# Layer 0 opens by pairs of channel tiles, and its modulation products run in four column groups of the array

## The chip, the cores and the metric

The kernel runs on one core of a Trainium2 chip. The metric is the device time of one execution in microseconds (us). Engines are named as in the profile: PE (matrix products), PEld (weight loads of PE), DVE and ACT (vector and scalar work), POOL, and SP, which issues most DMAs.

## The reference, cut to what matters

Two layers run over 1024 latent and 256 context tokens, 1024 channels wide. Each layer first derives a shift, a scale and a gate per channel from a conditioning vector, once for the latents (c) and once for the context (c_ctx), and modulates the normalised tokens with them. The result h feeds all the layer's projections: attention, a convolution branch, a recurrent branch (RG-LRU), and merge gates.

```python
shift, scale, gate = jnp.split(jax.nn.silu(c) @ w_ada[l] + b_ada[l], 3, axis=-1)
shift_c, scale_c, gate_c = jnp.split(jax.nn.silu(c_ctx) @ w_ada[l] + b_ada[l], 3, axis=-1)
h = layer_norm(x) * (1.0 + scale[:, None]) + shift[:, None]
hc = layer_norm(ctx) * (1.0 + scale_c) + shift_c
q, k, v, g_att, u_conv, g_conv, x_lru, g_lru = split_in_proj(h @ w_in[l])
...
g = jax.nn.sigmoid(h @ w_gate + b_gate).reshape(h.shape[:-1] + (N_BRANCH, D_MODEL))
```

`w_ada[l]` is 1024 x 3072, so silu(c) and silu(c_ctx) are two rows against 24 column tiles of 128: tiles 0 to 7 are the shift, 8 to 15 the scale, 16 to 23 the gate. These are the modulation products.

## The kernel before, in words

**Splitting.** The layer's large products keep float32 accuracy by splitting both operands into a high part in a reduced float format (hi) and the rest (lo), and running three products: hi by hi, hi by lo, lo by hi. A weight tile (`Wt`, lines 321 to 344) is 512 KB: SP loads it into one of two slots named `raw` (`NWL` is 2), ACT copies it to `whi`, DVE subtracts to get `wlo`. The slot is free once DVE has read it. The modulated tokens are held transposed, channels on partitions, as `hchi`/`hclo` (context, 256 columns) and `hlhi`/`hllo` (two latent tiles of 512 columns): eight channel tiles of 128 each. In the code these three token tiles are NT_C, NT_0 and NT_1.

**The opening** (`emit_h0`, lines 429 to 504). An explicit list `order` sets the recorded order. For the modulation of layer 0, 16 tiles `raw0` of w_ada (shift and scale, 2 KB runs) are loaded, and `ada_rows` multiplies them unsplit in float32: 2 stationary columns (`cs`: c and c_ctx), 512 moving columns, eight channel tiles accumulated into one PSUM tile `pa`, four groups in all. `ada_fin` copies the 2 x 512 result to `arow` on ACT and turns it into columns with four small products against `sel`. Ten tiles of x (two of context, eight of latents, 128 tokens each) are loaded and normalised (`norm_x`: two statistics, an aggregate and small operations on DVE, a power on POOL, one pass on ACT). `modulate` transposes one channel tile of one token tile on PE, applies scale and shift on ACT (`hf`), and splits it on ACT and DVE.

**The order of the work.** The recorded program is put in order per engine by the framework's scheduler; every engine then runs its own list strictly in order, and so does the DMA issue of SP. In `phase1` a driver with a cost table (`Driver`, `Meter`) decides in which order the streams of the layer are recorded; nine streams run side by side, among them `lru_in` (products of the recurrent branch), `gates` (24 merge-gate tiles) and `att_values`.

**Later modulation products** (`ada_pair`, lines 391 to 403). The stream `gates` of layer 0 calls it 16 times, once after each of the first 16 gate tiles, for two column tiles each: the four gate pairs of layer 0 and the twelve pairs of layer 1. It takes two `Wt` units (so two loads, two ACT splits, two DVE splits) and runs 16 products with 4 stationary columns (`csr`, the hi and lo of `cs`) and 256 moving columns.

Of the kernel before, what the change touches and what calls it, by code (L numbers as in the profile page):

```python
# [8 lines left out]
F32 = mybir.dt.float32  # L9
# [3 lines left out]
ALU = mybir.AluOpType  # L13
# [176 lines left out]
def kernel(  # L190
# [25 lines left out]
    PR = ctx.enter_context(tc.tile_pool(name="padr", bufs=1, side="right"))  # L216
    pad(PR, 320, "padr")
# [39 lines left out]
    def load_rows(l, get):  # L257
# [3 lines left out]
        for off, n, src in (  # L261
# [11 lines left out]
            sp.dma_start(out=ra[off:off + n], in_=src)  # L273
        sp.dma_start(out=rb[0:CK * 4], in_=conv_dw_w[l].rearrange("k (r p) -> (k r) p", p=128))
# [81 lines left out]
    cs = K.tile([128, KD, 2], F32, tag="cs", name="cs")  # L356
    csr = K.tile([128, KD, 4], F32R, tag="csr", name="csr")
    sel = K.tile([4, 2], F32, tag="sel", name="sel")
    dve.tensor_tensor(out=sel, in0=ident[0:4, 0:2], in1=ident[0:4, 2:4], op=ALU.add)

    def load_c():
        rows = SM.tile([128, 128], F32, tag="crow", name="crow")
        sp.dma_start(out=rows[0:8], in_=c[0].rearrange("(r p) -> r p", p=128))
        sp.dma_start(out=rows[8:16], in_=c_ctx.rearrange("(r p) -> r p", p=128))
        t = SM.tile([128, 128], F32, tag="crow2", name="crow2")
# [6 lines left out]
        split(cs, csr[:, :, 0:2], csr[:, :, 2:4])  # L372
# [18 lines left out]
    def ada_pair(l, jj, row):  # L391
# [9 lines left out]
        for w in ws:  # L401
            w.free()
# [20 lines left out]
    hT, hr = {}, {}  # L423

# [3 lines left out]

    def emit_h0(R, P):
        tiles = [(ctxt, 0), (ctxt, 128)] + [(x, 128 * i) for i in range(8)]  # L430
        raws, xt = {}, {}
        nts = (NT_C, NT_0, NT_1)

        def load_x(i):
            t = R.tile([128, 2, 512], F32, tag="raw0", name="x0", bufs=17).rearrange("p a b -> p (a b)")
            sp.dma_start(out=t, in_=tiles[i][0][0, tiles[i][1]:tiles[i][1] + 128, :])
            xt[i] = t

        def load_ada(g, q):
            raws[g, q] = R.tile([128, 2, 512], F32, tag="raw0", name="raw0", bufs=17)  # L440
            sp.dma_start(out=raws[g, q], in_=w_ada[0][q * 256:q * 256 + 256, g * 512:g * 512 + 512].rearrange(
                "(k p) n -> p k n", p=128))

        rows_ = {}

        def ada_rows(g, q):
            if q == 0:
                rows_[g] = P.tile([128, 512], F32, tag="p0", name="pa", bufs=4)
            for k in range(2):
                pe.matmul(out=rows_[g][0:2], lhsT=cs[:, q * 2 + k, :], rhs=raws[g, q][:, k, :],  # L450
                          start=(q == 0 and k == 0), stop=(q == 3 and k == 1))
            if q == 3:
                ada_fin(0, [g * 4 + i for i in range(4)], rows_[g], 2,
                        R.tile([128, 512], F32, tag="hf0", name="arow", bufs=5))
# [8 lines left out]
        def modulate(j, nt):  # L463
# [5 lines left out]
            hf = R.tile([128, 512], F32, tag="hf0", name="hf0", bufs=5)  # L469
# [3 lines left out]
            if j < (4, 4, 6)[ti]:  # L473
                act.activation(out=hi, in_=hf[:, 0:n], func=AF.Copy)
            else:
                dve.tensor_copy(hi, hf[:, 0:n])
            dve.tensor_tensor(out=lo, in0=hf[:, 0:n], in1=f32(hi), op=ALU.subtract)

        load_c()
# [4 lines left out]

        def rows_tile():
            return R.tile([128, 128], F32, tag="rows", name="rows", bufs=2)

        order = [("a", 0, 0), ("a", 0, 1), ("a", 0, 2), ("r",), ("a", 2, 0), ("a", 0, 3), ("a", 2, 1), ("a", 2, 2),
                 ("a", 2, 3), ("x", 0), ("x", 1), ("a", 1, 0), ("a", 1, 1), ("a", 1, 2), ("a", 1, 3), ("a", 3, 0),
                 ("a", 3, 1), ("a", 3, 2), ("a", 3, 3), ("m", NT_C, 0), ("m", NT_C, 4), ("x", 2), ("x", 3),  # L490
                 ("x", 4), ("x", 5), ("x", 8), ("m", NT_0, 0), ("m", NT_0, 4), ("x", 6), ("x", 9), ("x", 7),
                 ("m", NT_1, 0), ("m", NT_1, 4)]
        for what, *v in order:
            if what == "m":
                for j in range(v[1], v[1] + 4):
                    modulate(j, v[0])
            elif what == "r":
                load_params(0, *load_rows(0, rows_tile))
            elif what == "a":
                load_ada(*v)  # L500
                ada_rows(*v)
            else:
                load_x(*v)
                norm_x(*v)
# [20 lines left out]
    def phase1(l, R, RH):  # L525
        last = l == DEPTH - 1
        full = [NT_0, NT_1] if last else [NT_C, NT_0, NT_1]
        allt = [NT_C, NT_0, NT_1]
        lo_t = C if last else 0
        p, d = prm[l], drv[l]  # L530
        sl, hl_, pl_ = Pool_(NS), Pool_(NHF), Pool_(4)
        state = dict(lru=False, late=False)

        def slot(name, dt=F32):
# [950 lines left out]
```

## Time and profile before

| | |
|---|---|
| median of 3 runs | 2303.75 us (2302.42 to 2304.94) |
| profiled execution, its own time | 2301.99 us |
| its span, first to last instruction | 2300.2 us |
| mean granted clock of PE | 0.991 of full speed |
| PE busy | 2248.0 us (98%) |
| DVE busy | 1681.1 us (73%) |
| ACT busy | 1005.0 us (44%) |

The time is read against PE: it is busy nearly throughout, so a change counts by the PE time that it adds or removes, and by the stretches in which PE waits or runs at a lower granted clock. A float32 product shows as two MATMUL rows in the profile, each with a weight load of its own.

### The profile page before, as it was taken

To read this page: it belongs to the slowest core of one execution; us is meant where nothing else is said; L and a number is where in the kernel's file an instruction comes from. 1 tells how busy PE (TensorE), PEld (TensorE's weight loads), DVE (VectorE), ACT (ScalarE), POOL (GpSimd) and SP (SyncE) were. 2 spreads that over 40 slices of the span, in tenths; PEclk is the share of its full clock that TensorE was granted. 3 is DMA by queue.
4 is the path that set the end of the run, shared out by engine and by line. 5 is a ranking of instruction groups with operands and counts; after the bars stand their busy time and mean duration, and the time that the engine had idled before them with its cause. 6 is when DMAs were issued, how large, how long until landed. Compare 5 with 4: busy or idle time off the path is not lost.

```text
span 2300.2 us, 29966 instructions
## 1 busy us (share of the span) xinstructions
PE 2248.0 (98%) x11344; PEld 1870.5 (81%) x11344; DVE 1681.1 (73%) x2453; ACT 1005.0 (44%) x1642; POOL 86.0 (4%) x140
## 2 busy tenths in 40 slices
PE   7999999999999999999999999999999999999998
PEld 2888888888888787888888788888888878878886
DVE  5579967868959875544678749879778797765667
ACT  3555563245444475421132544665243446642110
POOL 1000000000000111000001100000000011000002
PEclk8999999999999999999999999999999999999999
DMA  7223323433334232555461312224433334347532
GB/s 276 77 74 101 115 70 125 147 108 113 100 108 140 81 117 88 187 166 178 144 222 65 103 53 79 77 78 144 130 102 100 88 110 133 124 141 223 162 127 92
DMA packets 270945, 279.90 MB, mean 122 GB/s; under 512 B 19768, under 2 KB 199888, under 8 KB 270800
## 3 DMA queue, kind: packets, MB, share of 16 engines
q1 hardware_dynamic: 242288, 226.06, 31.6%
q10 hardware_dynamic: 28512, 51.92, 6.4%
q8 instruction: 89, 1.46, 0.3%
q14 instruction: 56, 0.46, 0.1%
HBM read 203.04 MB, written 74.88 MB: 121 GB/s over the span
## 4 chain that ended last, share of the span: by engine, by line
PE 90%; DVE 4%; ACT 2%; DMA 2%; issue 1%; SPq 0%; POOLq 0%; POOL 0%; ACTq 0%; DVEq 0%
PE ps L73 83%; PE yp L73 3%; PE pt L73 2%; PE pa L73 2%; DVE acc L73 1%; DVE P L73 1%; DMA qd<-qd 1%; DVE wlo L73 0%; DVE pl L73 0%; ACT whi L73 0%; PE p L73 0%; DVE xp L73 0%; DMA raw<-in_w_in_dram 0%; ACT hf L73 0%; DMA yst<-yd 0%
## 5 line engine op out<-in xcount | busy, mean ns | idle before, releaser
L73 PE MATMUL ps<-hlhi,whi 128*128 128x512 f32 x1728 | 681.5, 395 | 2.5 <-DVE pl L73 1.5
L73 PE MATMUL ps<-hllo,whi 128*128 128x512 f32 x1728 | 677.8, 392 | 0.0
L73 PE MATMUL ps<-hlhi,wlo 128*128 128x512 f32 x1728 | 677.1, 393 | 0.0
L73 PEld LDWEIGHTS ps<-hlhi,wlo 128*128 128x128 f32 x1728 | 325.8, 189 | 67.9 <-issue 0.4
L73 PEld LDWEIGHTS ps<-hlhi,whi 128*128 128x128 f32 x1728 | 326.3, 189 | 66.8 <-DVE pl L73 2.9
L73 PEld LDWEIGHTS ps<-hllo,whi 128*128 128x128 f32 x1728 | 326.2, 189 | 62.0 <-issue 0.2
L73 DVE SCALAR_TENSOR_TENSOR acc<-u,cwt,acc 128x1296 f32<-128x1296 f32 (+1 forms) x240 | 342.1, 1425 | 2.2
L73 ACT ACTIVATE whi<-raw 128x1024 fp32r<-128x1024 f32 x180 | 190.0, 1058 | 339.8 <-PE ps L73 307.2
L73 DVE TENSOR_TENSOR wlo<-raw,whi 128x1024 fp32r<-128x1024 f32 x180 | 220.6, 1226 | 96.5 <-ACT whi L73 93.5
L73 PE MATMUL ps<-yy,whi 128*128 128x512 f32 (+1 forms) x960 | 271.4, 368 | 2.5 <-DVE m L73 2.5
L73 PEld LDWEIGHTS ps<-yy,whi 128*128 128x128 f32 x960 | 173.7, 188 | 33.3 <-DVE m L73 3.1
L73 PE MATMUL ps<-yy,wlo 128*128 128x512 f32 (+1 forms) x480 | 176.5, 368 | 0.0
L73 ACT ACTIVATE ph<-pt 128x512 fp32r<-128x512 f32 x160 | 94.2, 593 | 144.2 <-PE pt L73 142.7
L73 DVE TENSOR_TENSOR pl<-pt,ph 128x512 fp32r<-128x512 f32 x160 | 109.3, 686 | 59.2 <-ACT ph L73 57.7
L73 PE MATMUL ps<-hchi,whi 128*128 128x256 f32 x480 | 135.9, 283 | 1.3 <-ACT whi L73 0.6
L73 PE MATMUL ps<-hchi,wlo 128*128 128x256 f32 x480 | 135.5, 282 | 1.0 <-DVE wlo L73 1.0
L73 PE MATMUL ps<-hclo,whi 128*128 128x256 f32 x480 | 134.8, 281 | 0.0
L73 ACT ACTIVATE P<-P,nm 128x640 f32<-128x640 f32 (+1 forms) x128 | 101.9, 798 | 73.1 <-DVE nm L73 72.5
L73 DVE CUSTOM_DVE_ANT_0 P<-ps,m_mid,nsink 128x640 f32<-128x640 f32 (+1 forms) x112 | 93.6, 860 | 43.6 <-PE ps L73 42.0
L73 ACT ACTIVATE tg<-ps,drv 128x512 f32<-128x512 f32 (+1 forms) x120 | 76.5, 638 | 69.0 <-PE ps L73 68.5
L73 PEld LDWEIGHTS ps<-yy,wlo 128*128 128x128 f32 x480 | 90.5, 188 | 15.2
L73 PE MATMUL pt<-ident,P 128*128 128x128 f32 x640 | 98.0, 273 | 3.3 <-DVE pl L73 1.4
(205 smaller groups left out, 3397.6 us busy)
## 6 DMA issues: line engine op xcount, KB each, us to landing
raw<-in_w_in_dram SPq DMA_DIRECT2D x60, 512.0 KB
raw<-in_w_ada_dram SPq DMA_DIRECT2D x48, 512.0 KB
raw<-in_w_gate_dram SPq DMA_DIRECT2D x48, 512.0 KB
th<-tg ACTq DMA_DIRECT2D x96, 256.0 KB
thl<-th SPq DMA_DIRECT2D x96, 256.0 KB
yd<-gs ACTq DMA_DIRECT2D x48, 256.0 KB
yst<-yd SPq DMA_DIRECT2D x48, 256.0 KB
raw<-in_w_branch_dram SPq DMA_DIRECT2D x24, 512.0 KB
```

Source lines behind the costliest of these rows:

```text
L73: return f(*a, **k)
```

## The change

It has three parts.

1. **The opening is reordered.** Loads of x come first, the parameter rows are loaded from ACT's DMA queue (`load_rows(..., act)`), and w_ada is read in four groups of two channel tiles (shift and scale together, 256 columns each, so 1 KB runs, eight loads of 256 KB per group). The list `order` is gone: group after group, `modulate` runs for two channel tiles of all three token tiles.
2. **Four accumulations of the layer begin in the opening** (`share`): the first `lru_in` weight tile against all three token tiles, and the first gate tile against NT_0, each three products per channel tile, as soon as that channel tile is there. `phase1` then finds these four PSUM tiles finished and only evacuates them. All of the high parts in `modulate` are now made on ACT.
3. **All modulation products are unsplit float32 in four column groups.** `csz` holds `cs` padded with zeros to 32 columns; channel tile k goes to columns 32(k mod 4) of the array, so four partial sums stand on four groups of 32 partitions, and `sel` (now 128 x 2) adds them. In `ada_pair` this removes the two `Wt` units: the pair loads its two tiles (`araw`) straight into the two slots `raw` and reads them there, so a slot is free only when PE has run the pair's products.

```diff
@@ emit_h0, lines 440 to 543 of the changed kernel
+        def load_ada(g):
+            for q in range(4):
+                raws[g, q] = R.tile([128, 2, 2, 256], F32, tag="raw0", name="raw0", bufs=18)
+                src = w_ada[0][q * 256:q * 256 + 256, 0:2 * D].rearrange("(k p) (t n) -> p k t n", p=128, t=2)
+                for k in range(2):
+                    sp.dma_start(out=raws[g, q][:, k], in_=src[:, k, :, g * 256:g * 256 + 256])
+        def ada_cols(g):
+            pa = P.tile([128, 512], F32, tag="p0", name="pa", bufs=4)
+            for k in range(KD):
+                c_ = k % 4
+                pe.matmul(out=pa[32 * c_:32 * c_ + 32], lhsT=csz[:, k, :],
+                          rhs=raws[g, k // 2][:, k % 2].rearrange("p t n -> p (t n)"), start=(k < 4), stop=(k >= 4),
+                          tile_position=(0, 32 * c_))
+            row = R.tile([128, 512], F32, tag="arow", name="arow", bufs=1)
+            act.activation(out=row, in_=pa, func=AF.Copy)
+            for i in range(4):
+                pe.matmul(out=pa[:, 2 * i:2 * i + 2], lhsT=row[:, i * 128:i * 128 + 128], rhs=sel4, start=True, stop=True)
...
+        def share(j, nt):
+            for kind in ("lru", "gate"):
+                if (kind, nt[0]) in first:
+                    w, ps = first[kind], first[kind, nt[0]]
+                    for i, (a, b) in enumerate(((0, 0), (0, 1), (1, 0))):
+                        pe.matmul(out=ps[:, 0:nt[2]], lhsT=w[a][:, j, :], rhs=hT[0, nt[0]][b][:, j, :],
+                                  start=(j == 0 and i == 0), stop=(j == KD - 1 and i == 2))
...
+        for g in range(4):
+            if 0 < g < 3:
+                load_ada(g + 1)
+            if g:
+                ada_cols(g)
+            for nt in nts:
+                if g == 0 and nt is NT_1:
+                    for i in range(6, 10):
+                        norm_x(i)
+                for j in (2 * g, 2 * g + 1):
+                    modulate(j, nt)
+                    share(j, nt)
@@ ada_pair
-        ws = [Wt(w_ada[l][i * 512:i * 512 + 512, jj * 128:jj * 128 + 256].rearrange("(k p) n -> p k n", p=128), 4, 256)
-              for i in range(2)]
         ps = psum()
-        for k in range(KD):
-            for v in range(2):
-                pe.matmul(out=ps[0:4, 0:256], lhsT=csr[:, k, :], rhs=ws[k // 4][v][:, k % 4, :],
-                          start=(k == 0 and v == 0), stop=(k == KD - 1 and v == 1))
-        ada_fin(l, [jj, jj + 1], ps, 4, row)
+        for i in range(2):
+            for g in range(4):
+                pe.matmul(out=ps[32 * g:32 * g + 32, 0:256], lhsT=csz[:, 4 * i + g, :], rhs=raws[i][:, g, :],
+                          start=(i == 0), stop=(i == 1), tile_position=(0, 32 * g))
+        ada_fin(l, [jj, jj + 1], ps, 128, row)
```

Two places show how the order moves. The first is PE in the opening of the changed kernel, at the second group of modulation products: `p` are transposes of x tiles (x_202 is the first context tile, x_334 to x_340 the last four of the latents), `pa` the modulation products, `ps` products of the layer.

```order
L73 MATMUL p_446<-ident,x_334 128x128
L73 MATMUL p_458<-ident,x_334 128x128
L73 MATMUL pa<-raw_261,cs 32x512 x2
L73 MATMUL pa<-raw_264,cs 32x512 x2
L73 MATMUL pa<-raw_267,cs 32x512 x2
L73 MATMUL pa<-raw_270,cs 32x512 x2
L73 MATMUL p_499<-ident,x_202 128x128
L73 MATMUL p_499<-ident,x_204 128x128
L73 MATMUL ps<-hlhi,whi 128x512
```

In the kernel before, the modulation products stand ahead of nearly all transposes; now the second group of four stands behind the transposes of the first of the last four latent tiles. On DVE of the changed kernel the factor `nb_410` that this x tile's normalisation needs (x_334) stands behind the statistics of x_338, two tiles later:

```order
L73 TENSOR_SCALAR rs_407<-mv_405 128x1
L73 BN_STATS st_424<-x0_338 128x6 x2
L73 BN_AGGR mv_416<-st_413 128x2
L73 SCALAR_TENSOR_TENSOR nb_410<-mv_405,rs_407 128x1
L73 BN_AGGR mv_427<-st_424 128x2
```

So the list of PE waits at this place for the load of x_338. The second place is the seventh modulation pair of layer 0, first on SP of the changed kernel (`araw` are the pair's two tiles, `raw` the layer's weight tiles; all share two slots), then on PE:

```order
L397 DMA araw_3150<-in_w_ada_dram 128x4x256
L397 DMA araw_3152<-in_w_ada_dram 128x4x256
L965 DMA vd0_142<-vh_2934 128x512
L965 DMA vd1_143<-vh_2938 128x512
L330 DMA raw_3188<-in_w_in_dram 128x8x128
L330 DMA raw_3194<-in_w_gate_dram 128x8x128
```

```order
L73 MATMUL ps_3032<-hlhi_185,wlo_2616 128x512
L73 MATMUL ps_3155<-araw_3150,cs_155 32x256 x4
L73 MATMUL ps_3155<-araw_3152,cs_155 32x256 x4
L73 MATMUL ps_3168<-ident_76,pj_3007 128x128 x4
L73 MATMUL ps_3155<-sel_157,arow_3154 128x2 x2
L73 MATMUL ps_3214<-hchi_179,whi_3190 128x256
L73 MATMUL ps_3214<-hclo_180,whi_3190 128x256
L73 MATMUL ps_3214<-hchi_179,wlo_3191 128x256
```

The load of `raw_3188` takes the slot of `araw_3150`, which PE's four products of that tile set free; `whi_3190` and `wlo_3191` are its split, and PE reads them nine small instructions later.

## Rows read from the trace of the kernel before

**Rows 1.** The page, part 1: busy time, share of the span and instructions.
```profile
PE 2248.0 (98%) x11344; PEld 1870.5 (81%) x11344; DVE 1681.1 (73%) x2453; ACT 1005.0 (44%) x1642; POOL 86.0 (4%) x140
```

**Rows 2.** Stretches of the opening: length, busy time per engine, PEclk, DMA share, GB/s.
```profile
0.00:10.00 10.00, 3.87 (x6) 0.78 (x7) 1.56 (x11) 1.81 (x3) 2.80 (x15) 1.00 0.49 164
10.00:20.00 10.00, 10.00 (x24) 1.90 (x23) 4.70 (x29) 0.80 (x2) 0.00 (x0) 1.00 0.88 314
20.00:30.00 10.00, 9.98 (x35) 3.16 (x34) 4.02 (x17) 2.96 (x3) 1.07 (x2) 1.00 1.04 393
30.00:40.00 10.00, 10.00 (x33) 2.91 (x32) 3.78 (x10) 0.59 (x1) 0.55 (x1) 1.00 1.05 389
50.00:60.00 10.00, 8.05 (x41) 6.88 (x40) 8.23 (x24) 10.00 (x15) 2.29 (x3) 0.55 0.52 157
```

**Rows 3.** Timeline of PE, opening: start, length, tile, shape, count, idle and releaser.
```profile
6.38 7.70 PE L73 MATMUL pa<-raw,cs 128*2 128x512 f32 x12 [0.27 <-DVE cs L73]
14.38 7.03 PE L73 MATMUL pa<-raw,cs 128*2 128x512 f32 x16
...
36.35 1.05 PE L73 MATMUL pa<-sel,arow 2*128 2x2 f32 x8
...
46.28 1.14 PE L73 MATMUL p<-ident,x 128*128 128x128 f32 x4 [1.76 <-ACT hf L73]
...
73.73 0.60 PE L73 MATMUL p<-ident,x 128*128 128x128 f32 x4
```

**Rows 4.** One stretch, instructions that read hchi, then those that read hlhi.
```profile
55.60:74.40 18.80, 7.38 (x32) 5.88 (x32) 0.42 (x1) 0.00 (x0) 0.91 0.30 92
55.60:74.40 18.80, 6.51 (x19) 3.78 (x20) 10.43 (x19) 5.86 (x10) 0.91 0.30 92
```

**Rows 5.** Groups on PE: tiles, shape, count, busy us, mean ns, idle before.
```profile
L73 PE MATMUL pa<-raw,cs 128*2 128x512 f32 x64 | 31.0, 633 | 0.3 <-DVE cs L73 0.3
L73 PE MATMUL ps<-whi,csr 128*4 128x256 f32 x128 | 31.6, 278 | 0.0
L73 PE MATMUL ps<-sel,arow 4*128 4x2 f32 x64 | 9.6, 251 | 0.2 <-ACT arow L73 0.2
```

**Rows 6.** Timeline of PE: two rows of one modulation pair, then the layer's products.
```profile
97.59 0.28 PE L73 MATMUL ps<-wlo,csr 128*4 128x256 f32 x1
...
98.29 0.28 PE L73 MATMUL ps<-wlo,csr 128*4 128x256 f32 x1
...
75.10 0.39 PE L73 MATMUL ps<-hlhi,wlo 128*128 128x512 f32 x1
...
76.02 0.39 PE L73 MATMUL ps<-hlhi,whi 128*128 128x512 f32 x1
```

**Rows 7.** Timeline of DVE and ACT: statistics and normalisation of one tile of x.
```profile
37.71 1.23 DVE L73 BATCH_NORM_STATS2 st<-x 128x6 f32<-128x512 f32 x2
...
42.36 1.23 ACT L73 ACTIVATE x<-x,nb,rs 128x1024 f32<-128x1024 f32 x1
```

**Rows 8.** Split of a weight tile: instructions, ns min/median/max, first and last start.
```profile
L73 ACT ACTIVATE whi<-raw x180: 1039/1061/1081, 46.6 to 2211.0; 128x1024 fp32r<-128x1024 f32 x180
L73 DVE TENSOR_TENSOR wlo<-raw,whi x180: 1207/1220/1996, 48.4 to 2215.9; 128x1024 fp32r<-128x1024 f32 x180
```

**Rows 9.** Timeline of SP and ACT: one weight load, from issue to its split.
```profile
95.45 0.37 SPq L332 DMA_DIRECT2D raw<-in_w_in_dram  x1
...
100.25 1.06 ACT L73 ACTIVATE whi<-raw 128x1024 fp32r<-128x1024 f32 x1 [0.21 <-DMA raw<-in_w_in_dram]
```

**Rows 10.** PE's longest wait from 75 to 745 us; that stretch by engine.
```profile
PE yp L73 <- ACT ph L73: 3.7, 4, 1.9
...
95.00:745.00 650.00, 642.51 (x3562) 544.97 (x3561) 525.21 (x692) 310.96 (x501) 2.01 (x17) 1.00 0.35 110
```

**Rows 11.** A gap of PE between the layers, and the granted clock around it.
```profile
1313.76 1.97 PE L73 MATMUL ps<-ident,xp 128*128 128x128 f32 x8 [3.87 <-ACT hf L73]
...
1310.00:1320.00 10.00, 6.24 (x22) 5.32 (x23) 6.18 (x11) 9.70 (x23) 1.13 (x5) 0.66 0.19 68
```

More of the change, by code (lines that the diff above doesn't have):

```diff
@@ L423 @@
     hT, hr = {}, {}
+    GATES = list(range(16, 24)) + list(range(8, 16)) + list(range(8))
     def alloc_h(ti, n):
@@ new lines, in ada_cols @@
+        def ada_cols(g):
[9 more added lines that the diff above has]
+                pe.matmul(out=pa[:, 2 * i:2 * i + 2], lhsT=row[:, i * 128:i * 128 + 128], rhs=sel4, start=True, stop=True)
+            for part in range(2):
+                jj = 8 * part + 2 * g
+                bias = prm[0][:, P_ADA + jj:P_ADA + jj + 2].unsqueeze(2).to_broadcast([128, 2, 2])
+                dve.scalar_tensor_tensor(out=ada[0][:, jj:jj + 2, :],
+                                         in0=pa[:, 4 * part:4 * part + 4].rearrange("p (m s) -> p m s", s=2),
+                                         scalar=float(part), in1=bias, op0=ALU.add, op1=ALU.add)
@@ L483, in emit_h0 @@
                 pad(H, 64, "padh2")
[L485 to L504, printed above, removed]
+        ra, rb = load_rows(0, lambda: R.tile([128, 128], F32, tag="rows", name="rows", bufs=2), act)
+        for i in range(2):
+            load_x(i)
+        load_ada(0)
+        load_params(0, ra, rb)
+        for i in range(2, 6):
+            load_x(i)
+        for i in range(2):
+            norm_x(i)
+        first["lru"] = wcols(w_in[0], O_XL)
+        load_ada(1)
+        ada_cols(0)
+        for i in range(2, 6):
+            norm_x(i)
+        for i in range(6, 10):
+            load_x(i)
+        first["gate"] = wcols(w_gate[0], GATES[0] * 128)
+        for nt in nts:
+            first["lru", nt[0]] = psum()
+        first["gate", 1] = psum()
+        for g in range(4):
[3 more added lines that the diff above has]
+                ada_cols(g)
+            for nt in nts:
+                if g == 0 and nt is NT_1:
+                    for i in range(6, 10):
+                        norm_x(i)
+                for j in (2 * g, 2 * g + 1):
+                    modulate(j, nt)
+                    share(j, nt)
     class Pool_:
@@ L531, in phase1 @@
         sl, hl_, pl_ = Pool_(NS), Pool_(NHF), Pool_(4)
+        if first:
+            pl_.take(4)
         state = dict(lru=False, late=False)
@@ L619, in lru_in @@
                 for nt in allt:
-                    yield from gemm_nt(w, nt, evac)
+                    if ("lru", nt[0]) in first:
+                        yield "act"
+                        evac(first.pop(("lru", nt[0]))[:, 0:nt[2]], nt)
+                        pl_.give()
+                    else:
+                        yield from gemm_nt(w, nt, evac)
                 w.free()
@@ L1101, in att_out @@
                 yield from gating(0, j, get, 1.0)
-        gorder = list(range(16, 24)) + list(range(8, 16)) + list(range(8))
+        gorder = GATES
         def gate_nt(w, j, nt):
@@ L1117, in gates @@
         def gates():
-            ws = {}
+            ws = {0: first.pop("gate")} if l == 0 else {}
             def fetch(i):
```

82 lines of the change are left out of this document (39 added, 43 removed).

## The prediction, made before the changed kernel ran

> **What bounds the kernel now.** I read first the page's busy times: PE is busy 98% of the span, DVE 73%, ACT 44% [rows 1]. So the layer's products set the time, and a change pays by PE time saved or by gaps closed. Then the opening in stretches: for 40 us the DMAs are the tight resource, 164 and 314 GB/s in the first two stretches, then 393 and 389 at a busy share over 1 [rows 2]; PE counts as busy there, but with modulation products. Its timeline shows what they cost: 16 rows take 7.03 us, so (7.03 - 0.59) / 15 = 0.43 us a row, and there are 64 rows for 32 products [rows 3, 5]. Each float32 product is thus two passes of 0.43 us. The first twelve rows took 7.70 us, where 12 x 0.43 is 5.2: the clock came up on the way, 2.5 us lost [rows 3].
>
> The last transposes of x end at 74.3 us [rows 3]. By then PE had run products of the layer: 32 readers of hchi, which are two in three, so 48 of 256 columns, and likewise 29 of 512 [rows 4]. A 256-column row starts every (98.29 - 97.59) / 6 = 0.117 us, a 512-column row every 0.92 / 4 = 0.23 [rows 6]; that makes 5.6 + 6.7 = 12.3 us of useful work. The opening therefore costs 74.3 - 12.3 = **62 us** in which no product of the layer ran. After it PE hardly waits: from 95 to 745 us it is idle 7.5 of 650 us [rows 10].
>
> **The change, part by part.**
>
> *The price of the four column groups* is the unknown on which most hangs; no row before uses them. Bounds: all four at once (a group of eight products, 16 passes, takes 4 passes' time), or one after another (16). I take 9: a product is two passes on the same columns, so its second pass waits for its first; rows of PE start in order, so the next product's first pass can only run beside that second one. Sixteen passes then take 9 slots of 0.43 us at 512 columns, of 0.215 at 256 (half the columns).
>
> The Trainium skill (TensorE: Matmul & The Clock Gate, Part 3) says that matmuls start and end in program order, which is the step I lean on; it also measured 2.38 times for three column tiles, which speaks for a gain near the first bound. No run here shows either.
>
> *The opening.* Until the last x tiles are there PE can do little. In the new order PE's second modulation group stands behind transposes of x_334, these behind its normalisation, whose factor stands on DVE behind the statistics of x_338. Up to x_338, 9 tiles of x, one weight tile and two modulation groups are loaded: (9 + 1) x 0.52 + 2 x 2.1 = 9.4 MB. Before, 20 us brought 4.8 MB and the rest would come at 0.39 MB per us [rows 2], so at 32 us; but eleven small loads no longer stand on SP among the large ones, and at the full rate from 2.5 us on it is 27. I take 28. Statistics (1.23), small operations (0.5) and the normalisation (1.23) follow [rows 7]: 31 us. From there PE has, beside products of the layer:
> - three modulation groups of 9 x 0.43: 11.6 us (bounds 5.2 and 20.6);
> - 68 of 80 transposes at (0.60 - 0.27) / 3 = 0.11 [rows 3]: 7.5 us;
> - three sets of `sel` products at 1.05 [rows 3]: 3.2 us;
> - a clock that must rise once more: PE had granted 0.55 where it waited in the opening [rows 2]; 2.5 us as above;
> - two waits for ACT's `hf` of 1.76 us as shown [rows 3], since the third and fourth groups' factors come late in PE's list: 3.5 us.
>
> That is 28.3 us. Of the products begun in the opening, 12 rows on the first two channel tiles (6 of 256, 6 of 512 columns: 2.1 us) lie before 31 us. So the opening now costs 31 - 2.1 + 28.3 = 57.2 us against 62: **-5 us** (ends: -12 and +4). The 19 us of products that `share` brings forward are no gain in themselves; they only fill gaps. ACT's pass for the remaining high parts and the parameter loads lie beside the DMA stretch; ACT, busy all of 50 to 60 us before [rows 2], is the next to be late, which is why I keep the two waits.
>
> *The 16 pairs.* Before, 16 rows of 0.117: 1.87 us. Now 9 x 0.215 = 1.93: **+1 us** in all. The `sel` products stay at four rows a pair [rows 5]. Bounds: 4 slots, -16 us; 16 slots, +25 us.
>
> *ACT and DVE work removed*: 32 splits, 1.06 us on ACT and 1.22 on DVE each [rows 8], 34 and 39 us. PE's idle time in that stretch is 7.5 us in all, the longest group of waits 3.7 us behind ACT [rows 10]; so between 0 and -7.5, and I take **-2 us**, since most waits belong to attention, not to queues.
>
> *The wait that is added.* A pair holds both raw slots until PE has run it, and the next weight load on SP stands behind. A weight load took from its issue at 95.45 to its split at 100.25, 4.8 us [rows 9]; with 1.06 and 1.22 for the split [rows 8] the first product can start 5.9 us after the slot is free, the third 7.1. At the seventh pair PE has only four passes' worth of the pair (1.0), four transposes (0.45) and two `sel` products (0.5) before it reads that weight: 1.9 us. PE stands for 4 us, and 1 more for `wlo`. Following all 16 pairs down PE's list in the same way, one more is short (4.6 us of work, 2 us of wait); the others have 6.6 us or more. **+7 us** (ends: 0 if the scheduler's order hides more than I see; 12, since a PE gap of 3.87 us elsewhere went with a granted clock of 0.66 over 10 us [rows 11]).
>
> *Sum:* -5 + 1 - 2 + 7 = +1 on the profiled execution's 2301.99 (0.1% under the median, inside the spread of the runs): **2303 us**, no change. A measurement of this kernel can tell about 0.2%, 4.6 us, from nothing.
>
> **The rivals.**
>
> 1. *Four groups truly at once.* Three opening groups save 3 x 5 x 0.43 = 6.5 us, 16 pairs 16 x 5 x 0.215 = 17 us: 2303 - 23.5 = **2279**. For it: the four groups touch different columns and different partitions of PSUM. Against it: the two passes of each product on the same columns. The Trainium skill's 2.38 of 3 (the page and part named above) is of this kind.
>
> 2. *No overlap at all* (the side of slower). Then 16 passes stay 16: 3 x 7 x 0.43 = 9 us in the opening and 16 x 7 x 0.215 = 24 us in the pairs: **2336**. It decides from about 11 slots in place of 9 on: two slots more are 2 x (3 x 0.43 + 16 x 0.215) = 9.5 us, which is slower. For it: every row of the trace so far runs one pass after another. Against it: separate columns need nothing from each other.
>
> 3. *Each change between whole array and column groups empties PE.* A 256-column row lasts 0.278 us, one starts every 0.117 [rows 5, 6]; the difference, 0.16 us, is what an emptied pipeline loses. Two changes for each of 16 pairs and 4 groups: 40 x 0.16 = 6.4 us: **2309**. For it: nothing in the trace, where rows of 4 and of 128 stationary columns follow each other at the same pace. The Trainium skill (TensorEngine Tiling (Array Packing), Key Properties) states that changing the tiling mode drains the engine; no run here shows it.
>
> **How the numbers follow.** Chances: the forecast 0.38, rival 1 0.32, rival 2 0.17, rival 3 0.13. The forecast's own range, from its ends, is 2291 to 2316; rival 1 has 2268 to 2290, rival 3 2300 to 2320, rival 2 2322 to 2350. A range from 2270 to 2322 leaves out nearly all of rival 2 and the best edge of rival 1, about 2 in 10. Faster by over 0.2%: nearly all of rival 1 and a quarter of the forecast, 0.42. Within 0.2%: nearly half of the forecast and a quarter of rival 3, 0.21. Slower: the rest, 0.37.
>
> **What would show it.** In the changed profile: eight column-group products of a pair spread over 1.9 us (0.9 for rival 1, 3.4 for rival 2), with the next product of the layer 0.1 us behind (0.25 or more for rival 3); the second opening group starting near 31 us and the last transposes of x near 72; products of the layer done by then worth 14 us or more; a PE wait of 4 us or more on `whi` or `wlo` right behind the seventh pair, where before there was none. A last transpose at 65 us or earlier, or a pair under 1.5 us, breaks my sum downward; a pair over 2.5 us, or waits on weights of over 12 us in all, breaks it upward.

## The result, and the profile after

| | before | after |
|---|---|---|
| median of the runs beside each other | 2303.09 us (2300.58 to 2304.94, 4 runs) | 2333.68 us (2332.05 to 2335.93, 4 runs) |
| span of the profiled execution | 2300.2 us | 2333.4 us |
| mean granted clock of PE | 0.991 | 0.982 |

The change makes the kernel slower: the ratio is 1.0131, with an interval of 1.0117 to 1.0145. The forecast was no change. The busy times of the page, which answer to [rows 1]:

```profile
PE 2243.2 (96%) x11344; PEld 1865.7 (80%) x11344; DVE 1644.5 (70%) x2417; ACT 982.6 (42%) x1619; POOL 82.7 (4%) x139
```

PE is busy 4.8 us less than before, but idle 2333.4 - 2243.2 = 90.2 us where it was idle 52.2. So the time went into waits, not into work. The first place to look is the opening, in the stretches of [rows 2] that differ most:

```profile
20.00:30.00 10.00, 4.24 (x14) 2.62 (x14) 8.94 (x44) 7.61 (x10) 2.16 (x4) 0.50 1.09 361
30.00:40.00 10.00, 6.93 (x24) 2.68 (x24) 8.20 (x23) 6.31 (x8) 2.16 (x4) 0.50 1.09 349
```

PE waits there at half the clock, as foreseen. The timeline of PE shows the second group of modulation products, a later group, and the last transposes of x [rows 3]:

```profile
36.36 0.69 PE L73 MATMUL p<-ident,x 128*128 128x128 f32 x2 [2.02 <-ACT x L73]
36.98 3.53 PE L73 MATMUL pa<-raw,cs 128*32 128x512 f32 x16
...
49.17 1.92 PE L73 MATMUL pa<-raw,cs 128*32 128x512 f32 x16 [0.29 <-ACT hf L73]
...
69.83 1.68 PE L73 MATMUL p<-ident,x 128*128 128x128 f32 x12 [0.48 <-DVE ada L73]
```

The second group starts at 37 us, not 31. DVE shows why: the statistics of the first of the last four tiles (x_334) begin at 29.9 us, when its load lands, and the factor that ACT needs is made 5 us later, behind the statistics of two more tiles and two splits, where 1.7 us was priced.

```profile
29.91 1.29 DVE L73 BATCH_NORM_STATS2 st<-x 128x6 f32<-128x512 f32 x2 [0.23 <-DMA x<-in_x_dram]
...
34.93 0.10 DVE L73 SCALAR_TENSOR_TENSOR nb<-mv,rs 128x1 f32<-128x1 f32 x1
```

At full clock a group of 16 passes takes 1.92 us; the forecast had 3.9. The errors happen to cancel: the last transposes end at 71.5 us. By then 12 of the rows that read `hchi` and 36 that read `hlhi` have started, which in the way of [rows 4] are 18 x 0.117 + 54 x 0.23 = 14.5 us of the layer's products. The opening costs 57.0 us, against 62 before. That is no loss.

A modulation pair, in the timeline of PE [rows 6]:

```profile
100.24 0.28 PE L73 MATMUL ps<-hchi,whi 128*128 128x256 f32 x1
100.45 1.07 PE L73 MATMUL ps<-araw,cs 128*32 128x256 f32 x16
101.45 0.38 PE L73 MATMUL ps<-hclo,whi 128*128 128x256 f32 x1
101.67 0.28 PE L73 MATMUL ps<-hchi,wlo 128*128 128x256 f32 x1
```

Sixteen passes take 1.00 us from the first start to the next product's start; before it was 1.87, and 1.93 was forecast. A row of 256 columns otherwise starts every 0.117 us, so each edge of the pair costs 0.21 - 0.12 = 0.09 and 0.22 - 0.12 = 0.10 us more. Inside the pair the rows start in four waves of four, 0.22 to 0.24 us apart; within a wave each starts 7 ns behind the one before. The first wave (a view of 100.4 to 100.6 us):

```profile
100.45 0.42 PE L73 MATMUL ps<-araw,cs 128*32 128x256 f32 x4
```

The pairs are cheaper than before, so they aren't the loss either.

The loss is in the rest of layer 0's first phase. Here is the stretch from 75 to 1000 us, by engine, of the kernel before and then of the changed one (columns as in rows 2):

```profile
75.00:1000.00 925.00, 909.68 (x4981) 772.29 (x4980) 692.42 (x974) 450.32 (x758) 26.23 (x41) 0.99 0.35 111
```

```profile
75.00:1000.00 925.00, 880.96 (x4830) 741.47 (x4829) 639.82 (x912) 411.56 (x706) 23.70 (x38) 0.98 0.34 103
```

PE is idle 15.3 us before and 44.0 us after. The changed kernel's waits of PE in this stretch (total us, times, longest) answer to [rows 10]:

```profile
PE pt L73 <- ACT P L73: 7.7, 2, 4.7
PE ps L73 <- ACT whi L73: 6.1, 3, 3.7
PE ps L73 <- ACT qh L73: 5.3, 1, 5.3
PE yp L73 <- ACT ph L73: 5.2, 7, 1.6
PE yp L73 <- DVE pl L73: 4.9, 7, 1.6
```

The longest of the kernel before in the same stretch are shorter, and no wait of `pt` on `P` or of `ps` on `qh` is in its list:

```profile
PE yp L73 <- ACT ph L73: 4.8, 6, 1.9
PE yp L73 <- DVE pl L73: 2.8, 3, 2.4
```

One of the changed kernel's waits is the one that was foreseen. The timeline of all engines behind the seventh pair:

```profile
361.50 1.07 PE L73 MATMUL ps<-araw,cs 128*32 128x256 f32 x16
...
362.20 0.38 SPq L330 DMA_DIRECT2D raw<-in_w_in_dram  x1
...
366.27 1.06 ACT L73 ACTIVATE whi<-raw 128x1024 fp32r<-128x1024 f32 x1 [2.69 <-DMA raw<-in_w_in_dram]
...
367.38 0.39 PE L73 MATMUL ps<-hchi,whi 128*128 128x256 f32 x1 [3.69 <-ACT whi L73]
...
368.64 0.58 PE L73 MATMUL ps<-hchi,wlo 128*128 128x256 f32 x1 [0.76 <-DVE wlo L73]
```

Four us for `whi` and one for `wlo` were forecast; 3.69 and 0.76 came. A lower clock follows, as it did behind the gap of [rows 11]; in this view PE's busy time is followed by PEclk, DMA share and GB/s:

```profile
367.00:379.00 12.00, 9.99 (x54) 0.72 0.69 210
```

But the other waits belong to attention (`P`, `qh`, `ph`), whose instructions the change doesn't touch. Why they wait longer is what the runs had to find.

### The profile page after: what moved, and what is told of

It is laid out like the page before. It is cut to its first block, busy times and chain, and to the rows that moved or that the text cites. A ratio compares the mean times of both kernels' runs of the same rounds, so it can differ in the third digit from the quotient of the medians.

```text
span 2333.4 us, 29872 instructions
## 1 busy us (share of the span) xinstructions
PE 2243.2 (96%) x11344; PEld 1865.7 (80%) x11344; DVE 1644.5 (70%) x2417; ACT 982.6 (42%) x1619; POOL 82.7 (4%) x139
## 4 chain that ended last, share of the span: by engine, by line
PE 84%; DVE 6%; DMA 4%; ACT 3%; issue 2%; SPq 0%; POOL 0%; POOLq 0%; ACTq 0%; DVEq 0%
PE ps L73 79%; PE yp L73 3%; PE pt L73 2%; DVE acc L73 1%; DMA yst<-yd 1%; DMA raw<-in_w_gate_dram 1%; DMA raw<-in_w_ada_dram 1%; DVE wlo L73 1%; ACT whi L73 1%; DVE P L73 1%; DMA raw<-in_w_in_dram 0%; ACT P L73 0%; ACT hf L73 0%; DVE pl L73 0%; PE pa L73 0%
## 5 line engine op out<-in xcount | busy, mean ns | idle before, releaser
L73 ACT ACTIVATE whi<-raw 128x1024 fp32r<-128x1024 f32 x148 | 156.4, 1058 | 315.1 <-PE ps L73 240.5
L73 DVE TENSOR_TENSOR wlo<-raw,whi 128x1024 fp32r<-128x1024 f32 x148 | 181.8, 1229 | 90.1 <-ACT whi L73 87.1
L73 DVE TENSOR_TENSOR pl<-pt,ph 128x512 fp32r<-128x512 f32 x160 | 109.0, 685 | 58.8 <-ACT ph L73 57.2
L73 PEld LDWEIGHTS pt<-ident,P 128*128 128x128 f32 x640 | 80.2, 143 | 35.0 <-ACT P L73 8.3
```

Source lines behind the costliest of these rows:

```text
L73: return f(*a, **k)
```

## The experiments

In every group the kernel before ran on the same chip; its median was between 2303.6 and 2304.8 us. "PE idle" is 925 us less PE's busy time from 75 to 1000 us in that kernel's trace.

| run | what it is | median us | ratio to before (interval) | PE idle |
|---|---|---|---|---|
| e1_own | change, pairs in slots of their own | 2314.76 | 1.0048 (1.0033 to 1.0063) | 32.2 |
| e1b_half | change, pairs in quarter tiles of another pool | 2316.92 | 1.0055 (1.0040 to 1.0070) | 25.3 |
| e2_open | new opening alone | 2319.11 | 1.0066 (1.0051 to 1.0081) | 24.9 |
| e3_pairs | new pairs alone | 2314.33 | 1.0047 (1.0031 to 1.0064) | 26.8 |
| e4_plan | before, pair's planned length altered | 2322.73 | 1.0085 (1.0070 to 1.0100) | 26.9 |
| e5_own_plan | e1_own, planned length put right | 2298.68 | 0.9980 (0.9970 to 0.9989) | 21.2 |
| e6_pairs_own | new pairs alone, own slots, length right | 2316.88 | 1.0053 (1.0037 to 1.0070) | 31.4 |
| e7_hop | before, planner's constant 0.20 to 0.25 | 2333.12 | 1.0127 (1.0112 to 1.0142) | 36.7 |
| o6_pairs_own | e6_pairs_own in the choices of before | 2289.73 | 0.9936 (0.9919 to 0.9952) | 11.2 |
| o1_own | e1_own in the choices of before | 2282.05 | 0.9904 (0.9889 to 0.9919) | 11.3 |
| o0_after | the whole change in the choices of before | 2283.41 | 0.9914 (0.9900 to 0.9929) | 15.0 |
| o2_open | e2_open in the choices of before | 2305.81 | 1.0012 (1.0003 to 1.0021) | 15.1 |
| v1_after_hop25 | the whole change, constant 0.25 | 2307.19 | 1.0014 (1.0003 to 1.0025) | 27.9 |
| v2_after_hop15 | the whole change, constant 0.15 | 2299.78 | 0.9984 (0.9974 to 0.9993) | 22.5 |
| v3_before_hop15 | before, constant 0.15 | 2333.54 | 1.0126 (1.0109 to 1.0143) | 35.4 |
| r_own_hop | e1_own in the choices of e7_hop | 2317.28 | 1.0060 (1.0043 to 1.0076) | 34.6 |
| k_const | before with one more 8-byte constant | 2312.90 | 1.0039 (1.0023 to 1.0054) | 16.4 |
| n_one_group | o1_own, pairs in one column group | 2322.40 | 1.0083 (1.0068 to 1.0098) | 9.5 |

### Which part of the change costs?

Two theories came first: S, that the held `raw` slots cost, and O, that the new opening does. Four kernels took the parts asunder. e1_own gives the pair's tiles a `whi` and a `wlo` buffer, counted as one weight unit:

```diff
+        wlive[0] += 1
-            raw = W.tile([128, 4, 256], F32, tag="raw", name="araw", bufs=NWL)
+            raw = W.tile([128, 4, 256], F32, tag=("whi", "wlo")[i], name="araw", bufs=NW)
...
+        wlive[0] -= 1
...
-                    yield ("pe", both(hl_.room(), lambda: pl_.used < 2))
+                    yield ("pe", both(wroom(), hl_.room(), lambda: pl_.used < 2))
```

> Edit: the two tiles of a modulation pair no longer take the two raw slots but one whi and one wlo buffer, which the pair counts as one weight unit; opening and column groups as changed. Theory S (the pairs hold both raw slots until PE has run them, so weight loads, and all that stands behind on SP, come late): the loss goes and the gains of opening and pairs stay, 2283 to 2297 us, PE waits on whi and on DMA-fed tiles in layer 0 under 5 us. Rival O (the new opening leaves the rest of layer 0 with a poorer order of streams): 2325 us or more, same waits.

e1b_half puts the pair's weights in four tiles of the pool of half tiles instead:

```diff
...
-            raw = W.tile([128, 4, 256], F32, tag="raw", name="araw", bufs=NWL)
+            raw = half("araw").rearrange("p (k n) -> p k n", k=2)
...
```

> Edit: the pair's 512 KB tiles lie in four buffers of the half pool instead of the raw slots; opening and column groups as changed. Theory S: 2283 to 2299 us, as the raw slots are free for weights, with a few us for the half buffers that other streams wait for. Rival O: 2325 us or more.

e2_open has the new opening and the old `ada_pair` with its two `Wt` units, 16 split products and `csr`:

```diff
...
-                pe.matmul(out=ps[32 * g:32 * g + 32, 0:256], lhsT=csz[:, 4 * i + g, :], rhs=raws[i][:, g, :],
-                          start=(i == 0), stop=(i == 1), tile_position=(0, 32 * g))
...
+                pe.matmul(out=ps[0:4, 0:256], lhsT=csr[:, k, :], rhs=ws[k // 4][v][:, k % 4, :],
+                          start=(k == 0 and v == 0), stop=(k == KD - 1 and v == 1))
...
```

> Edit: the new opening with its column groups, but the 16 later pairs as before (split, 4 columns, through the weight units). Theory S: the opening's 5 us are left, 2294 to 2301 us. Rival O: the loss comes with the opening, 2318 to 2345 us.

e3_pairs is the reverse: the opening of the kernel before, and the changed `ada_load` and `ada_pair`.

> Edit: the old opening, with the 16 pairs unsplit in column groups and loaded into the raw slots as in the change (a 320-byte pad is dropped and two small tiles move to the opening's pool, to make room for the padded columns). Theory S: the loss comes with the pairs, 2328 to 2345 us, with PE waits on whi behind pairs. Rival O: the pairs alone gain, 2290 to 2297 us.

**Measured:** 2314.8, 2316.9, 2319.1 and 2314.3. The opening alone costs 15 us and the pairs alone 10, together 25 of the 30; freeing the slots gives back 19 of the 30. Neither theory holds: only e2_open lies in a range that was expected, O's 2318 to 2345, and e3_pairs then speaks against O. Each part alone costs 10 to 15 us, also the pairs, which spare PE work. That points to something that every part disturbs: the order that the driver in `phase1` works out.

### Does the order by itself cost that?

The driver prices a float32 row at four times its columns. So it takes the changed pair for 3.41 us where PE needs 1.0, and took the old one for 1.71. Theory M says that this wrong length does it; theory R, that any other order would; theory F, that layer 0's first phase is held by loads and splits, so that whatever PE is spared it waits for. e4_plan tells the driver of the kernel before the wrong length, and e7_hop moves a constant that has nothing to do with the change. Neither adds or removes an instruction.

```diff
@@ e4_plan, ada_pair of the kernel before
+        pe.t += 16 * 256 / 2400.0
         ada_fin(l, [jj, jj + 1], ps, 4, row)
@@ e7_hop
-HOP = (0.2, 0.4, 0.1, 0.15)
+HOP = (0.25, 0.4, 0.1, 0.15)
```

> The kernel before, with one number of its planner altered: a modulation pair is written down as 3.41 us of PE (what the planner writes down for the changed pair, since it prices a float32 row at four times its columns), where it was 1.71. No instruction is added or removed; only the order written out for layer 0 can move. Theory M (the changed kernel's planner takes a pair for 3.41 us, PE needs 1.3 with the edges, so PE comes to the next products before their operands): the same lie told of the old pair costs 10 to 20 us, 2313 to 2325. Theory R (the constants of the planner fit the order of the kernel before; any other order loses, whatever moved it): 2308 to 2325. Theory F (layer 0's first phase is held by loads and splits, so PE time saved is waited away): no change, 2300 to 2308.

> The kernel before with the planner's hand-over time for layer 0's first phase at 0.25 us instead of 0.20: the same instructions, written out in another order from some 240 us on. Theory R: slower by 5 to 20 us like every other order, 2308 to 2325. Theories M and F: no change, 2300 to 2308.

e5_own_plan and e6_pairs_own tell the driver the right length, for e1_own and for the pairs alone:

```diff
+        pe.t -= 22 * 256 / 2400.0
         ada_fin(l, [jj, jj + 1], ps, 128, row)
```

> The changed kernel with the pair's weights in slots of their own (as in e1_own, 2314.8 us) and with the planner told 1.07 us for a pair instead of 3.41. Theory M: most of the loss that was left goes, 2285 to 2300. Theory R: another order, no better in kind, 2303 to 2325. Theory F: as e1_own, 2311 to 2318.

> The old opening; only the pairs are new, in four column groups, with their weights in slots of their own and 1.07 us written down for each in the plan. PE is spared some 0.65 us a pair, 10 us. Theory M: the gain is kept, 2288 to 2297. Theory R: the gain less what a new order loses, 2297 to 2315. Theory F: the gain is waited away, 2300 to 2308.

**Measured:** 2322.7 for e4_plan and **2333.1 for e7_hop**: a hand-over time of 0.05 us more, and the kernel before loses 29 us, as much as the whole change did. Theory F predicted no change for both, and falls. e5_own_plan came to 2298.7, as M had it, but e6_pairs_own to 2316.9 where M had 2288 to 2297, and for e7_hop M, like F, had no change. A right length doesn't give a good order. Of theory R what stands is that the order alone moves the time by tens of us, whatever moved it. Its ranges held for e4_plan only, and e5_own_plan, 16 us faster than e1_own by its order alone, shows that another order can also gain.

What a poorer order looks like, e7_hop's trace shows. First PE's waits from 75 to 1000 us, then the place of the 4.3 us one, by DVE, ACT and PE:

```profile
PE pt L73 <- ACT P L73: 5.6, 3, 2.9
PE ps L73 <- ACT qh L73: 4.7, 2, 3.4
PE ps L73 <- ACT xh L73: 4.3, 1, 4.3
```

```profile
253.23 1.55 DVE L73 SCALAR_TENSOR_TENSOR xc<-X,prm,xc 128x1284 f32<-128x1284 f32 x1
254.70 1.56 DVE L73 SCALAR_TENSOR_TENSOR acc<-u,cwt,acc 128x1296 f32<-128x1296 f32 x1
256.18 0.42 DVE L73 TENSOR_TENSOR gs<-gs,h 128x256 f32<-128x256 f32 x1
256.51 1.55 DVE L73 SCALAR_TENSOR_TENSOR xc<-X,prm,xc 128x1284 f32<-128x1284 f32 x1
...
258.10 1.27 ACT L73 ACTIVATE xh<-xc 128x1284 fp32r<-128x1284 f32 x1 [10.94 <-DVE xc L73]
```

```profile
254.71 0.39 PE L73 MATMUL ps<-hlhi,wlo 128*128 128x512 f32 x1
259.42 1.44 PE L73 MATMUL ps<-xh,lwh 128*128 128x260 f32 x3 [4.33 <-ACT xh L73]
```

DVE's list holds the taps of `xc` (recurrent branch) in turn with taps of `acc` (convolution), 1.5 us each; `xh` can start only behind the last tap of `xc`, and its products stand next in PE's list, with no other stream's work between. So PE stands for 4.33 us. In the kernel before, DVE's taps stand in turn just the same, and the last of `xc` is even later. But PE's list has other products up to 263 us, and PE doesn't wait. DVE, then PE, of the kernel before:

```profile
258.40 1.55 DVE L73 SCALAR_TENSOR_TENSOR xc<-X,prm,xc 128x1284 f32<-128x1284 f32 x1
```

```profile
263.18 0.39 PE L73 MATMUL ps<-hlhi,wlo 128*128 128x512 f32 x1
263.41 0.75 PE L73 MATMUL ps<-xh,lwh 128*128 128x260 f32 x3
```

### The same change in the choices of the kernel before

Now the driver chooses nothing: it takes the stream of each step from the list of choices that the kernel before made (1460 steps in layer 0's first phase, 355, 1116 and 213 in the others). With that list the kernel before comes out row for row as it was. A listed stream that cannot go yet is passed over for the next in the list that can: in o0_after, o1_own and o2_open that happens nine times, in o6_pairs_own never. Where the new opening leaves a step without work, an empty step stands.

```diff
-            pick = None
-            side = [s for s in open_ if s["kind"] != "pe" and self.t[s["kind"]] < tp + LEAD[self.phase]
...
+            pick = self.listed(live, open_)
```

> As e6_pairs_own (only the pairs new, their weights in slots of their own, 2316.9 us), but the planner no longer chooses: it takes the streams in the list of choices that the kernel before made. What is left of another order are local moves. Theory R (the lost time is the order's): what PE is spared by column groups is seen in full, 2290 to 2298. Theory F (layer 0's first phase is held by loads and splits): waited away, 2300 to 2308 or more.

> As e1_own (new opening and pairs, own slots, 2314.8 us) in the choices of the kernel before, with empty steps where the products begun in the opening need none. Theory R: the opening's 4 us and the pairs' 10 us are both kept, 2286 to 2295. Theory F: 2300 to 2308 or more.

> The whole change as it stands, pairs in the raw slots (2333.7 us), in the choices of the kernel before. Theory R: 14 us spared less the waits of the held raw slots (the seventh pair's 4.5 us and the half clock behind it, 3 us, and perhaps one or two more), 2294 to 2306. Theory S (holding the raw slots is itself the main loss, 15 us or more): 2308 to 2325.

> Only the new opening, pairs as before (as e2_open, 2319.1 us), in the choices of the kernel before. Theory R: the 4 us by which the same products were done sooner at 100 us stay, 2297 to 2303. Theory O (the new opening harms what follows, by the state it leaves queues and pools in): 2312 to 2322.

**Measured:** 2289.7, 2282.1, 2283.4 and 2305.8. The change as it stands takes 2283.4 us in these choices and 2333.7 in its own: **50 us lie in the order alone**, and the change itself is worth -20. Theory F falls once more, and so does S: in these choices the held slots cost 1.4 us in the medians (o0_after against o1_own). The page's busy times of o0_after and the stretch from 75 to 1000 us:

```profile
PE 2224.1 (97%) x11344; PEld 1855.0 (81%) x11344; DVE 1642.3 (72%) x2417; ACT 984.0 (43%) x1619; POOL 84.6 (4%) x139
```

```profile
75.00:1000.00 925.00, 910.02 (x5070) 771.47 (x5070) 663.28 (x953) 431.72 (x739) 26.09 (x42) 0.99 0.37 114
```

With the same instructions as the changed kernel PE is idle 15.0 us instead of 44.0, and busy 19 us less in all. Most of the 19 goes with the mean granted clock, 0.988 against 0.982: by these means the time lost to the lower level is 0.012 x 2286 = 27 us against 0.018 x 2333 = 42. The wait for held slots is still there, at two other places. PE's waits of o0_after from 450 to 620 us:

```profile
PE ps L73 <- ACT whi L73: 5.6, 2, 3.2
PE ps L73 <- DVE wlo L73: 0.8, 1, 0.8
```

SP's queue is no measure of it. Its waits behind PE from 75 to 950 us are shorter by a quarter in o0_after, 209 against 272 us, as often and of the same kind, where the times are 50 us apart. The changed kernel, then o0_after (total us, times, longest):

```profile
SPq L330 <- PE ps L73: 271.5, 18, 45.1
```

```profile
SPq L385 <- PE ps L73: 208.8, 17, 35.1
```

Two misses were left. o0_after and o1_own came out below theory R's ranges, since the pairs are worth more than I had counted (14 us and not 10, and more still by what k_const shows below). And o2_open came out 3 us above its range.

### Is the order of the kernel before an exception? And the two misses

The next runs gave each kernel other orders, and took up the misses. v1_after_hop25, v2_after_hop15 and v3_before_hop15 are the edit of e7_hop with the values in their names. r_own_hop is e1_own in the list of choices of e7_hop.

> The whole change (2333.7 us) with the planner's hand-over time at 0.25 us instead of 0.20, nothing else: another order of the same instructions. Theory R1 (the order of the kernel before is a lucky one, the changed kernel's an ordinary one): 2310 to 2345, unlike 2333.7 by 5 us or more. Theory R2 (the planner's rules serve the changed kernel badly in one definite place): 2330 to 2337 again.

> The whole change with the planner's hand-over time at 0.15 us: one more order of the changed kernel, beside 2333.7 at 0.20, 2307.2 at 0.25 and 2283.4 in the choices of the kernel before. If the last is at the good end of what orders give: 2295 to 2340. If any order but the planner's at 0.20 would do: 2283 to 2295.

> The kernel before with the hand-over time at 0.15 us instead of 0.20. Theory R1: slower by 10 to 30 us as with 0.25 and as with the pair's altered price, 2312 to 2335. Theory R3 (0.25 happened to be a bad value and the kernel before keeps its time in most orders): 2298 to 2310.

> The changed kernel with own slots for the pairs in the bad order, that of the kernel before at 0.25 us (e7_hop, 2333.1 us), where in the order of the kernel before it took 2282.1. If order and change add up, 2333.1 less 21.5: 2306 to 2318. If the change is worth nothing in a poor order, since PE's time saved is waited away there: 2326 to 2340.

**Measured:** the kernel before at 0.15, 0.20 and 0.25 takes 2333.5, 2304 and 2333.1 us; the changed one 2299.8, 2333.7 and 2307.2. So the order of the kernel before is an exception among its neighbours, and the changed kernel's own order is the worst of its four (theory R1, though v1_after_hop25 came out 3 us below R1's range). Change and order add up roughly: in the poor order of e7_hop the change with slots of its own takes 2317.3, 16 us less than the kernel before took in that order, where the good order gave 22. All four changed orders average 2306 us; the kernel before's four (with e4_plan) 2323.

k_const asks why o2_open missed. The five kernels that hold the old constants and the new together (e2_open, e3_pairs, e6_pairs_own, o2_open, o6_pairs_own) had longer rows in layer 1's last stage. From one 512-column row of `yy` to the next they have 231.1 ns in the mean there, where the kernel before, the changed one and all others have 226.7 or 226.8.

```diff
     sel = K.tile([4, 2], F32, tag="sel", name="sel")
+    more = K.tile([4, 2], F32, tag="more", name="more")
+    dve.memset(more, 0.0)
```

> The kernel before with one more constant tile of 8 bytes a partition beside `sel`, written once and never read; the order of PE, ACT and SP is the same to the row. In five kernels that hold the old and the new constants together, each 512-column row of layer 1's last stage started every 231 ns, not 227 as in the kernel before. If the place of what is allocated behind the constants does it, rows of 231 ns there and 4 to 6 us more, 2307 to 2311; if it came with the new instructions, no change, 2301 to 2306.

**Measured:** 2312.9 us, 8 to 9 us more, somewhat over what was expected. Timeline of PE in that stage, the first and the last of nine rows that stand 3 rows apart, of the kernel before and then of k_const:

```profile
2109.82 0.39 PE L73 MATMUL ps<-yy,wlo 128*128 128x512 f32 x1
...
2115.26 0.39 PE L73 MATMUL ps<-yy,wlo 128*128 128x512 f32 x1
```

```profile
2109.80 0.40 PE L73 MATMUL ps<-yy,wlo 128*128 128x512 f32 x1
...
2115.40 0.40 PE L73 MATMUL ps<-yy,wlo 128*128 128x512 f32 x1
```

24 rows take 5.44 us before and 5.60 with the constant, 227 and 233 ns each; over the whole stage it is 226.7 and 231.1, as in the five kernels. The waits of layer 0's first phase hardly differ (16.4 us idle, not 15.3). PE has the same rows in the same order in both, so the two traces can be laid side by side: k_const is 4.5 us behind at 2033 us and 8.5 at the end. So about half of the loss arises from 2033 us on, where those rows are. Some 3 us arise between 480 and 690 us, and two executions can't tell those from chance.

The instructions being otherwise the same, this points to the place of the tiles behind the constant, and the five kernels carry it too. Which property of the place does it was not tried. It isn't what parts the orders: the changed kernel, o0_after, the kernel before and e7_hop all have 226.7 ns. The opening alone, measured against k_const, is worth 6 us (ratios 1.0012 and 1.0039). Another estimate is lower: if the parts simply add, o6_pairs_own (-14), o1_own (-22) and o2_open (+3) give about -3 for the opening, -19 for the pairs and +5 for the longer rows.

n_one_group asks what the column groups are worth:

```diff
-                pe.matmul(out=ps[32 * g:32 * g + 32, 0:256], lhsT=csz[:, 4 * i + g, :], rhs=raws[i][:, g, :],
-                          start=(i == 0), stop=(i == 1), tile_position=(0, 32 * g))
+                pe.matmul(out=ps[0:32, 0:256], lhsT=csz[:, 4 * i + g, :], rhs=raws[i][:, g, :],
+                          start=(i == 0 and g == 0), stop=(i == 1 and g == 3))
...
```

> As o1_own (2282.1 us), but a pair's eight products stand in one column group, one after another. In the changed kernel's trace the 16 passes of a pair in four groups took 1.07 us and about 0.1 more at each edge. If the groups' whole worth is overlap, 16 passes now take 16 x 0.215 = 3.4 us and the edges go: 16 pairs x 2.2 = 35 us more, 2310 to 2322. If the two passes of one product also overlap within a group (so that the groups are worth less), a pair takes 1.7 to 1.9 us and the time is 2290 to 2298.

**Measured:** 2322.4 us, 40 us more than o1_own and at the upper end of what was expected. A pair in the timeline of PE:

```profile
91.69 3.64 PE L73 MATMUL ps<-araw,cs 128*32 128x256 f32 x16
95.27 0.50 PE L73 MATMUL ps<-hllo,whi 128*128 128x512 f32 x1
```

and the pairs' group of instructions on PE (times, busy us, mean ns, idle before), of n_one_group and then of o1_own:

```profile
L73 PE MATMUL ps<-araw,cs 128*32 128x256 f32 x256 | 59.0, 381 | 0.0
```

```profile
L73 PE MATMUL ps<-araw,cs 128*32 128x256 f32 x256 | 18.4, 387 | 0.0
```

The difference, 40.6 us of PE, is the difference of the times. In one group a row of a pair starts every 0.216 us, so the 16 passes stand one behind another. Without the overlap between the groups the pairs would lose and not gain.

## Why the prediction was wrong

**The step that failed** is the one that isn't in the sum: it carries the waits of the kernel before over to the changed one ("after it PE hardly waits"), and adds one wait that it followed down the list. Those 7.5 us [rows 10] are a property of one order. The change makes the driver write another, in which PE waits 28.7 us more from 75 to 1000 us. In the choices of the kernel before the change is worth -20 us, in its own +30; the missing term is +50: some 29 us of waits (44.0 against 15.0), and 19 us by which PE's rows take longer. The text had looked at the new list for one kind of wait (weights behind a pair) and didn't ask what the other waits, of attention and of the recurrent branch, become in it.

**The price of the column groups** was the second failure, on the other side. The step "I take 9" slots out of 4 to 16 was wrong: 1.00 us for 16 passes is 4.7 slots of 0.215, and 1.92 us in the opening 4.5 of 0.43. The passes of one group do stand one behind another, as the reason given had it (0.216 us each in n_one_group). What failed is the next clause, that the following product's first pass can only run beside that second one: the rows start in waves of four, so the next three products start beside that first pass and don't wait for the second. Whether PE takes them out of their order there, or the passes stand in that order in its program, the trace doesn't say. The Trainium skill (TensorE: Matmul & The Clock Gate, Part 3) has 2.38 times for three column tiles; by n_one_group and the changed kernel four give 3.6 times here, (95.27 - 91.69) / 1.00, for float32 products of two passes each. I had weighed its rule of program order above its measurement, and this case goes with the measurement.

**The terms one by one.**

- *Opening*, -5 forecast: 57.0 us was the account in the changed kernel, 57.2 the forecast. Inside it, the second group started 6 us late and the groups at full clock took half of what was taken. So the sum came out right by luck. Between runs of one order it is worth -3 to -6 by the two estimates above.
- *Pairs*, +1, and *ACT and DVE work removed*, -2: together -14 in o6_pairs_own, which has the longer rows in it; without them about -19. The slots explain 16 x (1.87 - 1.00 - 0.2) = 11 us. What is left is more than the 2 us counted for the removed splits; no run told it apart.
- *The added wait*, +7: at the foreseen place it was 3.69 + 0.76 us where 4 + 1 was forecast. In the choices of the kernel before there are 6.4 us at two places, but the time is only 1.4 us more than without held slots. The mechanism was right; in that order its effect on the time was smaller.

**The range.** The forecast's own range, 2291 to 2316, is narrower than its ends add up to: -12 + 1 - 7.5 + 0 and 4 + 1 + 0 + 12 give 2284 to 2319. The 2333.7 lies beyond both.

**The rivals.** Rival 1 (groups truly at once, 2279) had the mechanism of the groups right, and comes within 5 us of the change in the kernel before's choices; it failed on the same missing term. Rival 2 gave the right side for a reason that n_one_group excludes: no overlap would have cost 40 us on PE, and PE's work fell. Rival 3 (emptying at each change): the edges of a pair cost 0.2 us, some 3 us in all, where 2 x 0.16 were priced. The Trainium skill (TensorEngine Tiling (Array Packing), Key Properties) says that changing the tiling mode drains the engine; the rows agree with a small price of that kind. Of the signs named in the prediction, the pair under 1.5 us broke the sum downward; "waits on weights of over 12 us" did not come (6.1 us on `whi`, 0.8 on `wlo`), since the waits that came were others.

That it was the order is shown, both ways: one list of choices takes the change from 2333.7 to 2283.4 us, and a constant that has nothing to do with the change takes the kernel before from 2304 to 2333. Why the driver finds a good order for the kernel before at 0.20, and at none of its neighbours, was not studied; three values of one constant were tried for each.

A version that beats both kernels is o1_own: the whole change, pairs in slots of their own, in the list of choices of the kernel before, 2282.1 us.

## What to carry to other kernels

Where a planner writes the order, a change has two prices, its own and that of the order that it provokes; replay the old choices with the new instructions to tell them apart, before looking for the guilty part. Alter one neutral constant of the planner first: the spread that it gives (29 us here) is what a part-by-part experiment can't see below. And an engine that is 98% busy and hardly waits may owe that to one tuned order, so a sum of removed and added work holds only as long as the order does.

## What the runs showed of the hardware

Four column groups of 32 overlap nearly fully for float32 products of two passes: 16 passes of 256 columns in 1.00 us against 3.58 in one group, with about 0.1 us at each edge to products on the whole array. The rows start in waves of four, 7 ns apart within a wave and 0.22 to 0.24 us from wave to wave, where in one group a row of a pair starts every 0.216 us.

A constant of 8 bytes a partition that nothing reads made 512-column rows in layer 1's last stage start every 231 ns in the mean instead of 227 (233 in the stretch shown). The kernel took 8 to 9 us more, of which some 4 us arose from 2033 us on, the order of PE being the same. In the built programs the weight and token tiles of the kernels with 227 ns all start 32 bytes past a multiple of 64; in k_const and the five with 231 ns most start at a multiple of 64. That goes together in all kernels run here; that it is the cause was not tested.
